# Twelve units of half products in the first feed-forward layer, four adaLN sums moved into the state-space groups, and part of the norm and the decays on the scalar engine

## The chip, the cores and the metric

The kernel runs on one core of a Trainium2 chip. The core has a matrix engine (TensorE, PE in the profile), a vector engine (VectorE, DVE), a scalar engine (ScalarE, ACT), GpSimd (POOL) and a queue engine that issues most of the transfers (SyncE, SP). Each runs its own list of instructions in order, and waits on semaphores for the others. The metric is device time in microseconds for one execution; less is better.

## The reference

A sequence of 512 tokens of width 1024 passes two layers. The first mixes tokens by a short gated convolution, the second by a Mamba-2 state-space mixer (SSD) with 8 groups of 4 heads. After each comes a SwiGLU feed-forward layer (FFN) of width 2816. Each of the four sub-layers is wrapped in RMS norms and adaLN vectors: shift, scale and gate, made from a conditioning vector c.

```python
mod = (jax.nn.silu(c) @ ada_w + ada_b).reshape(bsz, DEPTH, 2, 3, D_MODEL)
for i in range(DEPTH):
    shift, scale, gate = (mod[:, i, 0, k][:, None, :] for k in range(3))
    h = rmsnorm(x, norm_g[i, 0]) * (1.0 + scale) + shift
    y = short_conv_mixer(...) if i % 2 == 0 else ssd_mixer(...)
    x = x + gate * rmsnorm(y, norm_g[i, 1])
    shift, scale, gate = (mod[:, i, 1, k][:, None, :] for k in range(3))
    h = rmsnorm(x, norm_g[i, 2]) * (1.0 + scale) + shift
    gate_, up = jnp.split(h @ f_w_in[i], 2, axis=-1)
    x = x + gate * rmsnorm((jax.nn.silu(gate_) * up) @ f_w_out[i], norm_g[i, 3])
```

In the state-space mixer, h @ w_in gives z, the convolved x, B and C, and a step size dt; within chunks of 64 tokens the decay exp(cs_l - cs_s), masked to l >= s, weights C·B; y is multiplied by silu(z) and normalized per group: y * rsqrt(mean(y²) + eps) * norm_g.

## The kernel before

All products are float32 by three passes in a faster format: a value is split into a high and a low part (a copy on ScalarE, then a subtraction on VectorE), and high·high, high·low and low·high are summed in PSUM. Weights arrive from HBM in a staging tile (`wst`, `wsu`), are split into `whl`, and multiply the 512 tokens as moving data. A column tile of 128 outputs by 1024 inputs is a plain *chunk*: 8 x 3 = 24 matmuls of 128x512 (lines 285 to 287).

A *unit* (class Units, lines 577 on) does the same job for two column tiles with seven half-size products instead of eight (sums of weight blocks against sums of activation halves): 7 x 12 = 84 matmuls of 128x256 (line 654, into PSUM tiles sA, sB, sC). It needs sums of weight blocks: `fetch` (lines 599 to 612) issues per unit two loads into `sg`, three into `wsu` and two adding transfers on GpSimd's queue, and the unit before must have freed its staging tile.

The adaLN vectors are 12 sets of 1024 columns. Each set is eight 512 KB loads (`ada_st`, line 1004) with a multiply-add on VectorE for each (`ada_madd`, lines 122 to 127), a fold (L140), one small matmul with the constant `four` (`ada_fin`, L147, into PSUM tile `ada_ps`), four small additions on VectorE (L151), and for the gates a transposition through PSUM to DRAM and back (`put_gates`, L316 to L324).

In the first FFN, 6 units cover the first column tiles (12 of 44), and plain chunks in a loop over k the rest, with `sums(n)` steps (n multiply-adds) strewn in; then the down projection, `seq`. In the loop `x_load` also brings pieces for that projection. The second FFN has 16 units; in its units 0 to 8 `gate_late` makes the last set (its loads are L2249). The state-space mixer is a loop over groups g: VectorE, ScalarE and TensorE have their order written by hand. In one step of the loop TensorE projects columns of the group after (`nxt.project`, four chunks, `project_z`, two), transposes the current group's x (`xtok`), forms states and outputs (yo, yd), while VectorE applies convolution taps (L1678), subtracts the decays' arguments (`e_sub`, L1790, 16 small instructions), applies the norm of the group before (`root`, `norm`: ScalarE square root L1863, VectorE reciprocal L1867, L1870), splits weights (L231) and combines y (L1829 to L1832). The start of the loop's body, as it is written:

```python
conv2 = [nxt.project(i) for i in range(2)]
prev.root()
for q in range(2):
    cur.e_sub(q)
nxt.later[3][0]()
for q in range(2):
    cur.e_exp(q)
prev.norm()
next(conv2[0])
```

In the last group's step the output projection begins: its first 48 matmuls (L387) run while the group before is normalized, then come xtok and scores of the last group, and 48 more. T below counts from the start of a group's first chunk; 767.96 us is the one shown.

Of the kernel before, what the change touches and what calls it, by code (L numbers as in the profile page):

```python
# [16 lines left out]
P = 128  # L17
# [21 lines left out]
def trunk_kernel(  # L39
# [707 lines left out]
    ada_sets = [q0 * P for q0 in (16, 24, 32, 40, 48, 56, 64, 72, 80)]  # L747
# [4 lines left out]
    with ExitStack() as ph:  # L752
# [377 lines left out]
        UN1 = 6  # L1130
# [203 lines left out]
        with tc.manual_schedule(engines={PE_ENGINE, mybir.EngineType.SP, mybir.EngineType.Activation,  # L1334
# [6 lines left out]
            madds = ada_begin(6)  # L1341
# [111 lines left out]
            sums(3)  # L1453
# [4 lines left out]
            sums(3)  # L1458
# [25 lines left out]
            for k in range(k0, last + 1):  # L1484
                if k - k % 2 + 4 <= last:
                    load_pair_at(k - k % 2 + 4, k % 2)
                if k < k0 + 12:
                    x_load(*divmod(k - k0, 4))
# [13 lines left out]
                sums(1 if k in (k0 + 3, k0 + 8) else 2)  # L1502
# [19 lines left out]
            rows_g = put_gates(2, mm_ps)  # L1522
            next(rows_g)
# [15 lines left out]
            for q, item in enumerate(seq):  # L1539
# [6 lines left out]
                if q == 0:  # L1546
                    list(rows_g)
# [38 lines left out]
    with ExitStack() as ph:  # L1586
# [99 lines left out]
        class Group:  # L1686
# [96 lines left out]
            def e_sub(self, q):  # L1783

                e = self.e[:, 2 * q:2 * q + 2]
                for hh in range(2):
                    for cc in range(NCH):
                        sl = slice(cc * P, (cc + 1) * P)
                        hd = 4 * self.g + 2 * q + hh
                        dve.tensor_scalar(e[:, hh, sl], e[:, hh, sl], cs_tok[:, hd, cc:cc + 1], 0.0,  # L1790
                                          SUB, ALU.min)

            def e_exp(self, q):

                e = self.e[:, 2 * q:2 * q + 2]
                act.activation(e, e, AF.Exp)
# [64 lines left out]
            def root(self):  # L1861
                self.rg = t2("rg")
                act.activation(self.rg, self.ssg, AF.Sqrt, bias=eps_t, scale=1.0 / 256)  # L1863

            def norm(self):
                g = self.g
                dve.reciprocal(self.rg, self.rg)  # L1867
                for q in range(2):
                    y = ygs[2 * g + q]
                    dve.scalar_tensor_tensor(y, y, mng[:, 2 * g + q:2 * g + q + 1], self.rg, MUL, MUL)  # L1870

# [25 lines left out]
        with tc.manual_schedule(engines={PE_ENGINE, mybir.EngineType.Activation, mybir.EngineType.DVE}):  # L1897
            cur, nxt, nn = Group(0), Group(1), Group(2)
            nxt.weights(0)
            convs = [cur.conv(i, lead_ps[1 + i]) for i in range(4)]  # L1900
# [76 lines left out]
            for g in range(1, NG - 1):  # L1977
# [5 lines left out]
                for q in range(2):  # L1983
                    cur.e_sub(q)
                nxt.later[3][0]()
                for q in range(2):
                    cur.e_exp(q)
                prev.norm()
                next(conv2[0])
                next(conv2[0])  # L1990
                nxt.later[3][1]()
                nxt.weights(2)
                nxt.later[4][0]()
                next(conv2[1])
                cur.step_a()
                for q in range(2):
                    cur.e_mul(q)
                next(conv2[1])
                next(conv2[0])
                nxt.later[4][1]()  # L2000
# [10 lines left out]
                if nn:  # L2011
                    nn.weights(0)
                    nn.later[0][0]()
                cur.step_cc()
# [15 lines left out]

            prev, cur = cur, nxt
            next(parts[0])
            prev.root()
            for q in range(2):
                cur.e_sub(q)
            for q in range(2):
                cur.e_exp(q)
            prev.norm()
            ops = next(parts[0])
            for op in ops[:3]:  # L2040
                op()
            cur.step_a()
            for op in ops[3:]:
# [36 lines left out]
    with ExitStack() as ph:  # L2080
# [137 lines left out]
        with tc.manual_schedule(engines={PE_ENGINE, mybir.EngineType.SP, mybir.EngineType.Activation,  # L2218
# [19 lines left out]
            four = s1t[:, 6, 0:P]  # L2238
            make_four(four)

            def gate_late():

                st = [raw[:, 18 + 2 * b:20 + 2 * b, :].rearrange("p a b -> p (a b)") for b in range(2)]
                acc = s1t[:, 7:11, :].rearrange("p a b -> p (a b)")
                part = s1t[:, 6, P:P + 32]

                def load(k):
                    if k < KD:
                        dma(st[k % 2], ada_w[k * P:(k + 1) * P, 88 * P:96 * P])  # L2249

                load(0)
                load(1)
                yield
                for k in range(KD):
                    ada_madd(acc, st[k % 2], k)
                    load(k + 2)
                    yield
                ada_fold(acc, part)
                yield
                yield from ada_fin(88 * P, part)  # L2260
                yield from put_gates(3)

# [272 lines left out]
```

## Time and profile before

| what | us |
|---|---|
| median of three runs | 1335.93 |
| the runs | 1336.46, 1334.27, 1335.93 |
| profiled execution | 1334.83 |
| span of its profile | 1333.0 |

The span is one execution between the first and last instruction that the profiler saw; the rest of the profiled execution's time, 1.83 us, lies around it. Stages by the span's clock: convolution mixer to about 200 us, units of the first FFN about 250 to 308, its chunks 308 to 446, its down projection 453 to 548, state-space start from 590, groups 608 to 888 at 40 us each, output projection with the last group to 960, units of the second FFN 1032 to 1200, its remaining chunks and down projection to the end. Rows of a view have engine, line, operation and tiles as out<-in; a row of a timeline has start and length ahead of them.

### The profile page before, as it was taken

How to read it: one execution, taken by the hardware profiler on the slowest of the kernel's cores; microseconds unless marked ns; L12 is line 12 of the kernel's file. 1: busy time of each engine (PE TensorE's matmuls, PEld its weight loads, DVE VectorE, ACT ScalarE, POOL GpSimd, SP SyncE). 2: the span in 40 equal slices, each digit the busy share in tenths (PEclk: the TensorE clock that was granted, in tenths of full speed). 3: DMA queues.
4: the chain of work that ended last, by engine and by line, in shares of the span. 5: the costliest groups of instructions: out<-in, count | busy, mean ns of one | idle time of the engine just before them, and what ended most of it. 6: DMA issues, size and time to landing. Idle time of an engine off the chain costs nothing.

```text
span 1333.0 us, 19834 instructions
## 1 busy us (share of the span) xinstructions
PE 1314.0 (99%) x7653; PEld 1140.6 (86%) x7653; DVE 1049.6 (79%) x1627; ACT 662.4 (50%) x1084; POOL 99.5 (7%) x123
## 2 busy tenths in 40 slices
PE   8999999999999999999999999999999999999998
PEld 7788889998887788898888888888889999998886
DVE  5578767887876896769988989888678887776888
ACT  5333346453122565665554555554574545554665
POOL 0000000110000140000000000000001111100330
PEclk9999999999999999999999999999999999999999
DMA  9768651687898892414534243413343999869871
GB/s 311 235 199 255 226 171 41 180 220 240 280 300 277 240 182 64 130 33 145 159 111 138 70 140 111 143 64 126 104 126 80 237 237 235 209 174 287 178 137 63
DMA packets 209970, 228.53 MB, mean 171 GB/s; under 512 B 9668, under 2 KB 164180, under 8 KB 208852
## 3 DMA queue, kind: packets, MB, share of 16 engines
q1 hardware_dynamic: 191280, 187.88, 45.6%
q0 software_dynamic: 14448, 26.48, 11.4%
q10 hardware_dynamic: 4148, 12.90, 3.0%
q8 instruction: 60, 0.98, 0.3%
q14 instruction: 34, 0.28, 0.1%
HBM read 198.52 MB, written 2.24 MB: 151 GB/s over the span
## 4 chain that ended last, share of the span: by engine, by line
PE 74%; DMA 11%; DVE 8%; ACT 3%; issue 2%; SPq 2%; ACTq 0%; DVEq 0%; POOLq 0%
PE ip L285 10%; PE ip L287 10%; PE ip L286 10%; PE y L387 8%; PE sA L654 5%; PE cA L2215 4%; DMA wsu<-wsu 4%; DMA wst<-in_f_w_in_dram 4%; PE cA L1309 3%; PE sC L654 2%; PE li L285 2%; PE li L287 2%; PE li L286 2%; DVE ada_acc L127 2%; PE li L936 1%
## 5 line engine op out<-in xcount | busy, mean ns | idle before, releaser
L285 PE MATMUL ip<-h,whl 128*128 128x512 f32 x744 | 294.4, 396 | 0.8 <-ACT whl L1477 0.3
L287 PE MATMUL ip<-h,whl 128*128 128x512 f32 x744 | 290.7, 391 | 2.2 <-DVE whl L1478 2.1
L286 PE MATMUL ip<-h,whl 128*128 128x512 f32 x744 | 290.0, 390 | 0.0
L287 PEld LDWEIGHTS ip<-h,whl 128*128 128x128 f32 x744 | 139.7, 188 | 33.7 <-DVE whl L1478 4.4
L285 PEld LDWEIGHTS ip<-h,whl 128*128 128x128 f32 x744 | 139.8, 188 | 31.9 <-ACT whl L1477 2.3
L286 PEld LDWEIGHTS ip<-h,whl 128*128 128x128 f32 x744 | 139.9, 188 | 27.8
L654 PE MATMUL sA<-tq,whl 128*128 128x256 f32 x792 | 103.7, 285 | 3.4 <-DVE g L681 1.6
L231 DVE TENSOR_TENSOR whl<-wst,whl 128x1024 fp32r<-128x1024 f32 x70 | 84.8, 1219 | 24.7 <-ACT whl L230 24.7
L654 PEld LDWEIGHTS sA<-tq,whl 128*128 128x128 f32 x792 | 98.3, 192 | 5.7 <-DVE g L681 2.5
L387 PE MATMUL y<-whlo,ys 128*128 128x512 f32 x384 | 89.3, 392 | 0.0
L387 PEld LDWEIGHTS y<-whlo,ys 128*128 128x128 f32 x384 | 71.8, 188 | 15.8 <-issue 0.7
L127 DVE SCALAR_TENSOR_TENSOR ada_acc<-ada_st,csil,ada_acc 128x1024 f32<-128x1024 f32 x63 | 80.7, 1281 | 3.7 <-DMA ada_st<-in_ada_w_dram 2.9
L285 PE MATMUL li<-h,whl 128*128 128x256 f32 x288 | 83.3, 289 | 0.0
L287 PE MATMUL li<-h,whl 128*128 128x256 f32 x288 | 81.7, 284 | 0.0
L286 PE MATMUL li<-h,whl 128*128 128x256 f32 x288 | 81.6, 283 | 0.0
L230 ACT CAST whl<-wst 128x1024 fp32r<-128x1024 f32 x70 | 72.7, 1041 | 11.1 <-DMA wst<-in_f_w_in_dram 9.0
L617 DVE TENSOR_TENSOR whl<-wsu,whl 128x1024 fp32r<-128x1024 f32 x46 | 56.3, 1223 | 26.3 <-ACT whl L616 26.1
L1678 DVE SCALAR_TENSOR_TENSOR cu<-ip,cols,cu 128x511 f32<-128x511 f32 (+2 forms) x84 | 62.8, 747 | 3.9 <-ACT cu L1675 1.4
L2215 PE MATMUL cA<-whlo,ao 128*128 128x512 f32 x264 | 61.0, 390 | 0.4 <-DVE c L2448 0.2
L2215 PEld LDWEIGHTS cA<-whlo,ao 128*128 128x128 f32 x264 | 49.3, 188 | 11.5 <-ACT whlo L2180 1.2
L616 ACT CAST whl<-wsu 128x1024 fp32r<-128x1024 f32 x46 | 48.1, 1045 | 18.7 <-PE sB L654 7.8
L1228 POOL DMA_DIRECT2D sg<-sg x22 | 19.1, 870 | 486.4 <-DMA sg<-in_f_w_in_dram 297.6
(385 smaller groups left out, 2571.0 us busy)
## 6 DMA issues: line engine op xcount, KB each, us to landing
ada_st<-in_ada_w_dram SPq DMA_DIRECT2D x88, 512.0 KB, 5.4
wst<-in_m_w_in_dram SPq DMA_DIRECT2D x14, 1024.0 KB, 5.6
wsu<-in_f_w_in_dram SPq DMA_DIRECT2D x24, 512.0 KB, 4.9
sg<-in_f_w_in_dram SPq DMA_DIRECT2D x44, 256.0 KB, 3.9
wsu<-in_f_w_in_dram SPq DMA_DIRECT2D x44, 256.0 KB, 5.2
wst<-in_f_w_in_dram SPq DMA_DIRECT2D x22, 512.0 KB, 6.1
wst<-in_f_w_in_dram SPq DMA_DIRECT2D x10, 1024.0 KB, 5.4
wst<-in_m_w_in_dram SPq DMA_DIRECT2D x20, 512.0 KB, 5.5
```

Source lines behind the costliest of these rows:

```text
L127: dve.scalar_tensor_tensor(acc, w, csil[:, k:k + 1], acc, MUL, ADD)
L230: later.append((lambda sw=sw, w=w: act.copy(w[:, 0, :nk, :], sw), lambda sw=sw, w=w: dve.tensor_tensor(w[:, 1, :nk, :], sw, w[:, 0, :nk, : ...
L231: lambda sw=sw, w=w: dve.tensor_tensor(w[:, 1, :nk, :], sw, w[:, 0, :nk, :].bitcast(F32), SUB)))
L285: pe.matmul(dst, w_at(w, 0, kk), a[:, 0, sl], start=start, stop=False)
L286: pe.matmul(dst, w_at(w, 0, kk), a[:, 1, sl], start=False, stop=False)
L287: pe.matmul(dst, w_at(w, 1, kk), a[:, 0, sl], start=False, stop=stop)
L387: pe.matmul(pst, a[:, al, tk], wt[:, wl, kk, :], start=k == 0 and i == 0, stop=k == K - 1 and i == 2, skip_group_check=bool(held))
L616: act.copy(dst[:, 0], src)
L617: dve.tensor_tensor(dst[:, 1], src, dst[:, 0].bitcast(F32), SUB)
L654: pe.matmul(dst, w[:, wl, k0 + k, :], self.moving(q, k, al), skip_group_check=True, start=q in self.FIRST and k == 0 and i == 0, stop=k == ...
L1678: dve.scalar_tensor_tensor(u[:, sft:], pst[:, :T - sft], w[3 - sft], u[:, sft:], MUL, ADD)
L2215: pe.matmul(bank[r][sub], a[:, al, q, tk], w[:, hl, q, :], start=first and k == 0, stop=last and k == 2, skip_group_check=True)
```

## The change

The first FFN now has 12 units (`UN1`), so the loop of plain chunks has 8 steps left, and x_load's pieces are issued in the first six of them. Nine adaLN sets were made in the first layer's FFN and before; now six are, with sums() steps reduced accordingly. The second FFN's `gate_late` is gone, as is the `put_gates(2)` ahead of the first FFN's down projection. The four sets of columns 64, 72, 80 and 88 (units of 128) are summed in groups 1 to 6 of the state-space loop, six steps to a group. A step is `late(g, 1)`: if a set has its fold, one step of its finish (`late_end`: first the small matmul, then the four additions, then the gate's transposition), then one multiply-add or fold.

```diff
-    ada_sets = [q0 * P for q0 in (16, 24, 32, 40, 48, 56, 64, 72, 80)]
+    ada_sets = [q0 * P for q0 in (16, 24, 32, 40, 48, 56)]
...
-        UN1 = 6
+        UN1 = 12
...
-            madds = ada_begin(6)
+            madds = ada_begin(3)
...
-            sums(3)
+            sums(2)
...
-                if k < k0 + 12:
-                    x_load(*divmod(k - k0, 4))
+                if k < k0 + 6:
+                    for i in (0, 2):
+                        x_load((k - k0) % 3, i + (k - k0) // 3)
...
-                sums(1 if k in (k0 + 3, k0 + 8) else 2)
+                sums(1)
...
-            rows_g = put_gates(2, mm_ps)
-            next(rows_g)
...
-                        dve.tensor_scalar(e[:, hh, sl], e[:, hh, sl], cs_tok[:, hd, cc:cc + 1], 0.0,
-                                          SUB, ALU.min)
+                        act.activation(e[:, hh, sl], e[:, hh, sl], AF.Relu, bias=cs_tok[:, hd, cc:cc + 1],
+                                       scale=-1.0)
...
-                act.activation(e, e, AF.Exp)
+                act.activation(e, e, AF.Exp, scale=-1.0)
...
-                act.activation(self.rg, self.ssg, AF.Sqrt, bias=eps_t, scale=1.0 / 256)
+                act.activation(self.rg, self.ssg, AF.Ln, bias=eps_t, scale=1.0 / 256)
+                act.activation(self.rg, self.rg, AF.Exp, scale=-0.5)
...
-                dve.reciprocal(self.rg, self.rg)
...
+        def late_sums():
+
+            held = ysp.tile([P, 2, T], F32, tag="ys", name="four")
+            for q0 in (64, 72, 80, 88):
+                acc, st = flat(ysp.tile([P, 2, T], F32, tag="ys", name="ada_acc")), []
+
+                def load(k):
+                    if k < KD:
+                        st.append(flat(ysp.tile([P, 2, T], F32, tag="ys", name="ada_st")))
+                        dma(st[k], ada_w[k * P:(k + 1) * P, q0 * P:q0 * P + D])
+
+                load(0)
+                load(1)
+                if q0 == 64:
+                    yield held[:, 0, 0:P]
+                for k in range(KD):
+                    ada_madd(acc, st[k], k)
+                    load(k + 2)
+                    yield
+                part = held[:, 1, q0 % 32:q0 % 32 + 32]
+                ada_fold(acc, part)
+                fins_late.append(late_end(q0, part))
+                yield
+
+        def late_end(q0, part):
+            yield from ada_fin(q0 * P, part)
+            if q0 % 24 == 16:
+                yield from put_gates(q0 // 24)
+
+        fins_late = []
+
+        def late(g, n):
+            for _ in range(n):
+                if fins_late and next(fins_late[0], 0) == 0:
+                    fins_late.pop(0)
+                next(steps_late, None)
...
                 prev.root()
-                for q in range(2):
-                    cur.e_sub(q)
+                late(g, 2)
                 nxt.later[3][0]()
-                for q in range(2):
-                    cur.e_exp(q)
                 prev.norm()
+                late(g, 1)
                 next(conv2[0])
                 next(conv2[0])
+                cur.e_sub(0)
                 nxt.later[3][1]()
...
                 next(conv2[1])
+                cur.e_sub(1)
                 cur.step_a()
+                late(g, 1)
+                for q in range(2):
+                    cur.e_exp(q)
...
             prev.root()
-            for q in range(2):
-                cur.e_sub(q)
-            for q in range(2):
-                cur.e_exp(q)
+            for step in fins_late:
+                list(step)
             prev.norm()
...
-            late = gate_late()
-            next(late)
...
-                    next(late, None)
```

The orders of the engines, at three places. First VectorE at the start of group 4 (the step of the loop in which the second set is finished), in the kernel before:

```order
L1850 TENSOR_TENSOR sqs<-accg,sqs 128x512
L231 TENSOR_TENSOR whl<-wst,whl 128x1024
L1790 TENSOR_SCALAR csb<-csb,cs_tok 128x128 x16
L1867 RECIPROCAL rg<-rg 128x512
L1870 SCALAR_TENSOR_TENSOR yg_7089<-yg_7089,cols_91,rg 128x512
L1870 SCALAR_TENSOR_TENSOR yg_7106<-yg_7106,cols_91,rg 128x512
L1678 SCALAR_TENSOR_TENSOR cu<-ip,cols_93,cu 128x511
```

and in the changed kernel (`ada_acc` is the sum, `mods` the finished vectors, `yg` the group's outputs):

```order
L1847 TENSOR_TENSOR sqs<-accg,sqs 128x512
L231 TENSOR_TENSOR whl<-wst,whl 128x1024
L125 TENSOR_SCALAR ada_acc<-ada_st,csil 128x1024
L151 TENSOR_TENSOR mods<-ada_ps,cols_92 32x8 x4
L127 SCALAR_TENSOR_TENSOR ada_acc<-ada_st,csil,ada_acc 128x1024
L1867 SCALAR_TENSOR_TENSOR yg_7072<-yg_7072,cols_91,rg 128x512
L1867 SCALAR_TENSOR_TENSOR yg_7089<-yg_7089,cols_91,rg 128x512
L127 SCALAR_TENSOR_TENSOR ada_acc<-ada_st,csil,ada_acc 128x1024
L1675 SCALAR_TENSOR_TENSOR cu<-ip,cols_93,cu 128x511
```

The decays' 16 subtractions and the reciprocal have left, and a first sum step, the four additions of the second set and further sum steps stand ahead of and around the norm. Second, TensorE in the same step; the rows are the end of its second chunk and what follows:

```order
L285 MATMUL ip<-h_5080,whl 128x512
L286 MATMUL ip<-h_5080,whl 128x512
L287 MATMUL ip<-h_5080,whl 128x512
L147 MATMUL ada_ps<-four 128x32
L1738 MATMUL xtok<-ident,xs_6479 128x128
L1738 MATMUL xtok<-ident,xs_6480 128x128
```

The set's small matmul L147, which the four additions read, stands behind the two chunks; in the kernel before, xtok follows the chunks directly. Third, VectorE where the output projection begins, before:

```order
L1881 TENSOR_TENSOR ys<-yg_6128,ys 128x512
L1790 TENSOR_SCALAR csb<-csb,cs_tok 128x128 x16
L1867 RECIPROCAL rg<-rg 128x512
L1870 SCALAR_TENSOR_TENSOR yg_7732<-yg_7732,cols_91,rg 128x512
L1870 SCALAR_TENSOR_TENSOR yg_7749<-yg_7749,cols_91,rg 128x512
L213 TENSOR_TENSOR whlo<-wsto,whlo 128x1024 x2
L1881 TENSOR_TENSOR ys<-yg_6437,ys 128x512
```

and in the changed kernel (`gcol` is the gate column, `ggp` its transpose in PSUM, `whlo` and `ys` the split weights and values of the second set of 48):

```order
L1915 TENSOR_TENSOR ys<-yg_6396,ys 128x512
L151 TENSOR_TENSOR mods<-ada_ps,cols_92 32x8 x4
L158 TENSOR_TENSOR gcol<-mods,cols_91 128x8
L322 COPY gr<-ggp 8x128
L1867 SCALAR_TENSOR_TENSOR yg_8106<-yg_8106,cols_91,rg 128x512
L1867 SCALAR_TENSOR_TENSOR yg_8123<-yg_8123,cols_91,rg 128x512
L213 TENSOR_TENSOR whlo<-wsto,whlo 128x1024 x2
L1915 TENSOR_TENSOR ys<-yg_6731,ys 128x512
```

The last set's additions, gate column and copy now stand between the projection's first values and the norm of the last group but one. On TensorE their matmul L147 and the transposition L319 follow the first 48 matmuls:

```order
L387 MATMUL y_8219<-whlo,ys 128x512 x3
L147 MATMUL ada_ps<-four 128x32
L319 MATMUL ggp<-ident,gcol 8x128
L1738 MATMUL xtok<-ident,xs_7527 128x128
L1738 MATMUL xtok<-ident,xs_7528 128x128
```

The transposition needs the gate column from VectorE, and xtok, the scores and the second 48 matmuls come behind it.

36 lines of the change are left out of this document (12 added, 24 removed).

## The prediction, as put on record before the result was known

> **What bounds the kernel now.** The page first: its head and the chain that ended last.
>
> ```profile
> span 1333.0 us, 19834 instructions
> PE 1314.0 (99%) x7653; PEld 1140.6 (86%) x7653; DVE 1049.6 (79%) x1627; ACT 662.4 (50%) x1084; POOL 99.5 (7%) x123
> PE 74%; DMA 11%; DVE 8%; ACT 3%; issue 2%; SPq 2%; ACTq 0%; DVEq 0%; POOLq 0%
> ```
>
> TensorE is busy for 99% of the span, so time is won only by taking matmuls away or closing its few holes, and lost wherever it is made to wait. The mean hides the stages that the change touches, so next the windows: the half-product units of both FFNs, the plain chunks of the first, one state-space group, and the output projection. Columns: window, length, busy time of PE, PEld, DVE, ACT, POOL, granted clock, DMA share, GB/s.
>
> ```profile
> 255.60:305.90 50.30, 49.69 (x411) 49.18 (x410) 42.66 (x57) 25.83 (x43) 7.79 (x9) 1.00 0.85 221
> 390.00:446.00 56.00, 53.22 (x226) 41.21 (x225) 40.76 (x48) 16.87 (x22) 0.00 (x0) 1.00 0.79 264
> 768.00:808.00 40.00, 40.00 (x217) 33.74 (x216) 35.63 (x59) 21.19 (x28) 1.30 (x1) 1.00 0.39 118
> 888.00:954.00 66.00, 65.97 (x327) 54.21 (x326) 52.59 (x77) 33.03 (x45) 0.00 (x0) 1.00 0.33 104
> 1095.00:1130.00 35.00, 32.69 (x265) 31.73 (x264) 28.70 (x39) 16.92 (x31) 5.19 (x6) 1.00 0.92 232
> ```
>
> Three things stand there. A state-space group (40.00 us) leaves no hole in TensorE, but VectorE has only 4.4 us to spare, while ScalarE has 18.8 and DMA more than half. The chunks of the first FFN leave TensorE holes at a DMA share of 0.79. And the units of the second FFN, at 0.92, leave holes too.
>
> **The change part by part.** *Chunks to units.* The prices are distances of starts in the timeline: two plain chunks in a row, and units (the last two rows are cut short by the window asked for).
>
> ```profile
> 767.96 0.39 PE L285 MATMUL ip<-h,whl 128*128 128x512 f32 x1
> 773.40 0.39 PE L285 MATMUL ip<-h,whl 128*128 128x512 f32 x1
> ...
> 1085.61 1.60 PE L654 MATMUL sB<-h,whl 128*128 128x256 f32 x12
> 1095.68 1.60 PE L654 MATMUL sB<-h,whl 128*128 128x256 f32 x12
> 1107.20 1.60 PE L654 MATMUL sB<-h,whl 128*128 128x256 f32 x12
> 1118.36 1.60 PE L654 MATMUL sB<-h,whl 128*128 128x256 f32 x12
> 1129.44 1.00 PE L654 MATMUL sB<-h,whl 128*128 128x256 f32 x7
> 1139.74 0.64 PE L654 MATMUL sB<-h,whl 128*128 128x256 f32 x4
> ```
>
> A chunk is 24 matmuls in 5.44 us, so the two that a unit replaces cost 10.88. An unhindered unit, 84 half-wide matmuls, takes 10.07 (1085.61 to 1095.68). That is 0.81 each and 4.8 us for six. But the next four took 11.52, 11.16, 11.08 and 10.30. What they waited for:
>
> ```profile
> 1088.05 0.37 SPq L605 DMA_DIRECT2D wsu<-in_f_w_in_dram  x1
> 1099.78 0.37 SPq L605 DMA_DIRECT2D wsu<-in_f_w_in_dram  x1
> 1099.87 1.05 ACT L616 CAST whl<-wsu 128x1024 fp32r<-128x1024 f32 x1 [3.62 <-DMA wsu<-wsu]
> ...
> 297.99 0.37 SPq L605 DMA_DIRECT2D wsu<-in_f_w_in_dram  x1
> 305.86 1.60 PE L654 MATMUL sB<-h,whl 128*128 128x256 f32 x12
> ```
>
> Weight fetches of successive units (L605) come 11.73 us apart, slower than the 10.07 that a unit takes, and 1107.20 and 1118.36 follow their fetches by 19.1 and 18.6 us: that is how long fetch, sum, cast and subtraction take. The first FFN's fetch at 297.99 would, at a full pace, belong to a unit at 305.86 + 10.07 = 315.93, 17.9 us behind: too short, so the loop decides from there. Those fetches carry one 512 KB adaLN load per unit (as the second FFN's did), and the new units 6 to 11 keep it. So I give these six units 11.25 us each, between 10.07 and 11.52. Twelve chunks now cost 65.3 plus holes; the window 390 to 446 has 222 plain matmuls, 222 x 0.227 = 50.3 us, and about 0.5 of adaLN, so some 5.1 of its 56 us are lost to DMA. The twelve chunks are 70.4 with these. Six units at 11.25 make 67.5, less 0.5 where the hole of the last plain chunk closes: **-3.4 us**. Bounds: units at 10.07 give 60.4 and -10; units at 11.73, the fetch distance itself, give 70.4 and no gain.
>
> *Second FFN.* Eight 512 KB loads and nine VectorE steps leave its units. Over the 10.07 pace those four units lose 1.45 + 1.09 + 1.01 + 0.23 = 3.8; the last of these may stay, so **-3.7** (from -2.5, the first two alone, to -4.3, with half a microsecond of the other units).
>
> *State-space groups.* What leaves and enters VectorE, and ScalarE's sequence at a group's start:
>
> ```profile
> 766.40 3.22 DVE L1790 TENSOR_SCALAR csb<-csb,cs_tok 128x128 f32<-128x128 f32 x16
> 771.42 3.35 DVE L1867 RECIPROCAL rg<-rg 128x512 f32<-128x512 f32 x1 [1.80 <-ACT rg L1863]
> 776.34 2.32 DVE L1678 SCALAR_TENSOR_TENSOR cu<-ip,cols,cu 128x511 f32<-128x511 f32 x3
> ...
> 769.40 1.28 ACT L1863 ACT_TABLE_LOAD   x1 [1.10 <-issue]
> 770.70 0.69 ACT L1863 ACTIVATE rg<-ssg,eps 128x512 f32<-128x512 f32 x1
> 772.34 1.28 ACT L1796 ACT_TABLE_LOAD   x1
> 773.63 2.01 ACT L1796 ACTIVATE csb<-csb 128x1024 f32<-128x1024 f32 x2
> ...
> L125 DVE TENSOR_SCALAR ada_acc<-ada_st,csil x9: 746/750/754, 72.3 to 419.0; 128x1024 f32<-128x1024 f32 x9
> L127 DVE SCALAR_TENSOR_TENSOR ada_acc<-ada_st,csil,ada_acc 128x1024 f32<-128x1024 f32 x63 | 80.7, 1281 | 3.7 <-DMA ada_st<-in_ada_w_dram 2.9
> L140 DVE TRANSPOSE_TENSOR_REDUCE fold<-ada_acc 128x32 f32<-128x1024 f32 x9 | 11.2, 1245 | 0.3
> L151 DVE TENSOR_TENSOR mods<-ada_ps,cols x40: 144/162/173, 110.2 to 1148.2; 32x8 f32<-32x8 f32 x40
> ```
>
> VectorE loses 3.22 + 3.35 = 6.6 us a group and gains six sum steps in groups 1 to 6: 5 x 1.28 + 0.75 = 7.2. From 35.6 it goes to 36.2, and 36.9 with a finish of a set (4 x 0.16). So far under 40: that alone is free. ScalarE gains 16 128x128 activations, between an eighth of the 1.0 us of a 1024-wide one and the whole 0.69 of the 512-wide one; at 0.3 each and one activation of 0.69 for the root, 21.2 becomes about 27, hidden too. The norm waits until load, logarithm, load and exponential are over, T = 5.4 us into the group by these rows (table load from 769.40, then 1.28 + 0.69 + 1.28 + 0.69), but its reciprocal ended at T = 6.8 (771.42 + 3.35): no loss.
>
> The Trainium skill, "ScalarE: Activation LUTs", section "What ACT_TABLE_LOAD costs", counts a drain of some 1.4 us to each load beside its 1.28; here the next activation starts right behind the load (772.34 + 1.28 = 773.62), so no run here shows it, and by the page the sum would be up to 1.4 us a group larger where the norm comes last.
>
> What costs is the finishing of a set, where an instruction stands at the wrong place of a strict sequence. In group 4 the finish's four L151 come second on VectorE, behind the first sum step, and they read the matmul L147. On TensorE that stands behind both chunks that the group begins with, that is 2 x 5.44 = 10.88 us into the group:
>
> ```profile
> 778.84 1.04 PE L1741 MATMUL xtok<-ident,xs 128*128 128x128 f32 x8
> 753.16 1.50 PE L1813 MATMUL yo<-ct,prev 128*128 128x128 f32 x12
> 754.59 1.97 PE L1824 MATMUL yd<-csb,xdt 128*64 128x128 f32 x32
> ...
>   PE ada_ps L147: 6.4, 1
> ```
>
> (778.84 is 10.88 behind 767.96; the last row, of what L151 waited for, shows that such a wait already happened once in the second FFN, 6.4 us.) Queued behind L151 are the norm, the taps of chunk 0 and all that follows. VectorE then does 0.75 us of work before T = 11.1 and 36.9 - 0.75 = 36.2 after it: the group ends at 47.3, **+7.3**. Bounds: +4, if groups 5 and 6 with 3 us of slack each recover part of it before TensorE notices, and +9.5 if the late loads behind it add 2. In group 2 the finish stands after the scores and costs nothing by itself, but the gate's transpose takes one of the auxiliary banks, and the copy that frees it stands far down VectorE's sequence: the second yd, ready at T = 27.6 (754.59 less 727.96, the group before, plus 1.0), gets its bank when y1 is read, T = 29.9: **+2.3** (0 to +3). In groups 1, 3 and 6 a sum step asks for a load that was issued only one step earlier: a few tenths each, +0.9 together, and 1.8 more that VectorE is late by when the output projection starts: **+2.7** (0 to +5).
>
> The tail, from the chain of waits:
>
> ```profile
> 888.16 10.88 PE y L387 x48
> 899.04 0.87 PE xtok L1741 x8
> 901.14 10.93 PE y L387 x48
> ```
>
> VectorE there normalizes the group before the last at 896.41, and the second set of y matmuls follows 4.73 us later.
>
> ```profile
> 896.41 1.41 DVE L1870 SCALAR_TENSOR_TENSOR yg<-yg,cols,rg 128x512 f32<-128x512 f32 x2
> ```
>
> Now the last set's finish comes ahead of that norm, and its L147 stands behind the 48 matmuls: 888.16 + 10.88 = 899.04, then matmul, four L151, gate column, transpose and copy, some 1.5 us at 0.2 to 0.3 for each that isn't an L151: norm at 900.6 and not 896.41, **+4.2** (+3 to +5).
>
> The groups together: 7.3 + 2.3 + 2.7 + 4.2 = **+16.5** (+11 to +19). The loads' own traffic is not the trouble there: 36 x 512 KB over 240 us add 79 GB/s to 118, where the window of the chunks moved 264.
>
> Sum: -3.4 - 3.7 + 16.5 = +9.4; against the profiled execution's 1334.83 that is 1344.2. The median of the runs shown is 1335.93, 1.1 above that execution, so the forecast is **1345.0 us**.
>
> **The rivals.** *VectorE's delay compounds, 1350* (chance 0.2). If group 4's delay makes loads of weights and decays late (they wait for buffers that VectorE frees), groups 5 and 6 lose some 2 us each, and the units run at the fetch distance of 11.73, no gain: 1345 + 2 + 3 = 1350. For it: six sum steps leave VectorE 3 us of slack only. Against it: the DMA share of 0.39.
>
> *The units keep their pace, 1338* (0.12). If fetches are no longer slowed by what surrounded them, the first FFN gains 10 and not 3.4: 1345 - 6.6 = 1338.4. For it: 255.60 to 305.90, with TensorE busy 49.69 of 50.30 and one sum load per unit from the third on. Against it: the fetch distance of 11.73 with just that load.
>
> *TensorE does not feel VectorE's delay, 1335* (0.08), the case that is not slower. VectorE's slack is 40 - 36.2 = 3.8 us in each group; over groups 4 to 6 that is 11.4, more than the 7.3 of group 4 and the 2.7 of the late loads. If TensorE's chunks, whose weights are split a chunk or more ahead, can stand in for the work that comes late, both terms vanish: 1345.0 - 10.0 = 1335.0. It decides from the point where a chunk's lead in weights exceeds the delay. For it: TensorE without a hole in the group. Against it: the matmuls of the states wait for xw and those of yo for prev, both made by VectorE behind the L151, and a chunk is only 5.4 us of cover.
>
> *The finishes hide entirely* (0.03), that is, the matmul L147 comes before the chunks on the chip: group 4 and the tail cost nothing, 1345 - 7.3 - 4.2 = 1333.5. Against it: TensorE runs its list in order in each view above.
>
> **How the numbers follow.** The forecast has 0.57; its own range, from the terms' bounds, is 1341 to 1348. With 1350 at 0.2, 1338 at 0.12 and 0.11 between 1333 and 1335, the range that holds eight in ten is 1336 to 1351. A measurement of this kernel can't tell less than 0.2%, 2.7 us, from no change, so "faster" means under 1333.3 and "slower" over 1338.6. Faster: half of the last rival, and four or five hundredths where two of the low cases meet, 0.06. Same: the rest of the last two rivals and most of 1338, half of which lies above the bound, 0.12. Slower: the forecast, 1350 and that half, 0.82.
>
> **What would show it.** In the profile after: L151 of group 4 idle for about 9 us on PE ada_ps; that group 47 us long, group 2 about 42, others 40 to 41; second y set 17 us behind the first, not 13; starts of the first FFN's units 11.2 us apart from the seventh on; no hole in the second FFN's units 7 to 10; ACT loads still three per group. Wrong it would be if the units of the first FFN lie 10.1 apart (then about 1338), or if TensorE's matmuls near the finishes show no wait longer than 2 us (then no more than 1335).

## The result and the profile after

| | before | changed |
|---|---|---|
| median, us | 1335.10 | 1347.33 |
| lowest to highest, us | 1332.97 to 1336.46 | 1345.70 to 1350.47 |
| runs | 4 | 4 |
| ratio to before, 95% interval | | 1.0096 (1.0072 to 1.0120) |
| profiled execution, span, us | 1333.0 | 1348.7 |

The changed kernel is slower by 12.2 us, and the time lies 2.3 us above the forecast. The profile shown is that of the changed kernel's longest execution, 1350.47 us; where the other profiles of nearly the same code differ, it is said. Its head and the chain that ended last:

```profile
span 1348.7 us, 20425 instructions
PE 1316.2 (98%) x7869; PEld 1152.9 (85%) x7869; DVE 1021.3 (76%) x1533; ACT 722.9 (54%) x1258; POOL 108.0 (8%) x135
PE 73%; DVE 11%; DMA 8%; ACT 4%; issue 3%; ACTq 0%; SPq 0%; POOL 0%; DVEq 0%; POOLq 0%
```

VectorE does 28 us less in all and stands on the chain for 11% of the span instead of 8%. It was relieved on average and became the last to arrive at a few places. The windows of the stages (columns as in the prediction): the sixth to the eleventh unit of the first FFN, group 4, the output projection with the last group, and the units of the second FFN that had holes.

```profile
306.00:376.00 70.00, 64.53 (x522) 62.81 (x521) 54.66 (x78) 32.62 (x56) 9.51 (x11) 1.00 0.87 221
771.80:819.50 47.70, 42.36 (x217) 35.24 (x217) 37.10 (x52) 26.18 (x44) 1.31 (x1) 0.96 0.56 168
891.50:957.00 65.50, 60.84 (x294) 48.81 (x293) 44.13 (x66) 38.67 (x63) 1.29 (x1) 0.97 0.28 94
1095.00:1150.00 55.00, 55.00 (x461) 55.00 (x460) 40.16 (x58) 28.67 (x49) 10.34 (x12) 1.00 0.86 215
```

The same work of a group, 217 matmuls, now takes 47.7 us with 5.3 us of holes, and ScalarE has gone to 26 us, about as estimated. The holes of the second FFN's units are gone.

All stages at once are told by the starts of a few TensorE instructions. The table has, from the timelines, the time from the first unit's sB to the first matmul of the down projection (cA) in each FFN, the steps from the xtok of group 0, 1, ... 6 to that of the next group, and the time from the last xtok to the last y. It holds the experiments too, which are described below.

| kernel | first FFN | steps of groups 0 to 6 | last group and projection | second FFN | span |
|---|---|---|---|---|---|
| before | 197.1 | 40.0, 40.0, 40.0, 40.0, 40.0, 40.0, 40.0 | 85.5 | 184.7 | 1333.0 |
| changed | 194.1 | 40.4, 44.5, 42.1, 40.5, 47.8, 40.3, 44.2 | 89.3 | 180.8 | 1348.7 |
| e1_group4 | 193.2 | 40.1, 44.8, 42.0, 41.1, 44.5, 40.3, 44.0 | 89.0 | 180.8 | 1344.0 |
| e2_tail | 192.2 | 40.2, 44.3, 42.0, 40.7, 49.0, 40.3, 44.3 | 87.5 | 180.8 | 1346.0 |
| e3_third | 194.6 | 40.0, 40.3, 42.1, 40.1, 47.6, 40.3, 42.7 | 89.0 | 180.8 | 1342.1 |
| e4_units | 189.5 | 40.6, 43.1, 42.0, 40.4, 49.0, 40.3, 45.7 | 88.3 | 180.8 | 1344.5 |
| e5_fins | 192.4 | 40.1, 40.2, 40.3, 40.2, 40.3, 40.3, 41.6 | 85.0 | 180.8 | 1325.6 |
| e6_all | 187.8 | 40.0, 40.3, 40.3, 40.2, 40.3, 40.3, 41.6 | 85.2 | 180.8 | 1321.5 |
| e7_dve | 191.0 | 41.9, 46.9, 44.3, 45.2, 43.8, 43.3, 45.9 | 85.1 | 180.8 | 1353.7 |

From before to changed the FFNs give 3.0 and 3.9 us, the seven steps of the groups take 19.8 more, and the last group with the projection 3.8 more. Another 1.1 us is gained between the first FFN's down projection and group 0, which no term of the forecast had and no run takes apart; what is left, 0.2, lies before and behind.

Where VectorE waited in the groups, the three largest sums (us in total, times, longest):

```profile
DVE mods L151 <- PE ada_ps L147: 19.0, 2, 9.8
DVE yg L1867 <- ACT rg L1861: 15.8, 5, 4.8
DVE ada_acc L127 <- DMA ada_st<-in_ada_w_dram: 6.1, 3, 3.1
```

The first line is the forecast's main term: two waits of over 9 us for the small matmul, one in group 4 and one in the last group. In group 4, VectorE's timeline, and TensorE's 16 us later:

```profile
772.27 0.75 DVE L125 TENSOR_SCALAR ada_acc<-ada_st,csil 128x1024 f32<-128x1024 f32 x1
782.86 0.69 DVE L151 TENSOR_TENSOR mods<-ada_ps,cols 32x8 f32<-32x8 f32 x4 [9.83 <-PE ada_ps L147]
...
802.52 0.49 PE L1810 MATMUL yo<-ct,prev 128*128 128x128 f32 x2 [3.67 <-DVE prev L1778]
```

The sum step, then 9.83 us of nothing, then the four additions. VectorE hardly stops after that, and 16 us later TensorE has run out of work that doesn't need it: yo waits 3.67 us for prev. In the last group the chain of waits runs right through the finish:

```profile
903.03 10.73 PE y L387 x46
913.76 0.15 PE ada_ps L147 x2
913.93 0.15 DVE mods L151
...
914.66 0.18 DVE gcol L158
914.84 0.04 issue
914.88 0.29 PE ggp L319
...
915.40 1.39 DVE yg L1867 x2
916.79 2.27 DVE whlo L213 x2
919.06 0.61 DVE ys L1915
919.67 0.04 issue
919.72 5.30 PE y L387 x15
```

Projection, small matmul, additions, gate column, transposition, norm, splits, projection: one behind the other, 16.7 us from the start of the first set (903.0; two matmuls of it went ahead at 901.5) to that of the second, where before it was 12.98.

Group 1 shows what the forecast priced too low, a late load. VectorE's third sum step there, and the piece of the chain ahead of it:

```profile
655.86 1.29 DVE L127 SCALAR_TENSOR_TENSOR ada_acc<-ada_st,csil,ada_acc 128x1024 f32<-128x1024 f32 x1 [3.14 <-DMA ada_st<-in_ada_w_dram]
...
646.68 0.37 SPq L221
647.16 8.61 DMA ada_st<-in_ada_w_dram
```

The load is issued right behind weights of the next group (L221, 1 MB) and lands after 8.6 us, where the median of these loads in the profile before is 5.4; everything on VectorE behind it moves by 3.1 us. Where the profile gives the landing of such a load in the groups, it took 3.5 to 12.0 us, 7.8 in the median. That the weights ahead of it are what makes this one late was not tested by itself.

### The profile page after: what moved, and what is told of

Its sections match the earlier page's. It is cut to its first block, busy times and chain, and to the rows that moved or that the text cites. A ratio compares the mean times of both kernels' runs of the same rounds, so it can differ in the third digit from the quotient of the medians.

```text
span 1348.7 us, 20425 instructions
## 1 busy us (share of the span) xinstructions
PE 1316.2 (98%) x7869; PEld 1152.9 (85%) x7869; DVE 1021.3 (76%) x1533; ACT 722.9 (54%) x1258; POOL 108.0 (8%) x135
## 3 DMA queue, kind: packets, MB, share of 16 engines
q0 software_dynamic: 16176, 29.63, 12.7%
## 4 chain that ended last, share of the span: by engine, by line
PE 73%; DVE 11%; DMA 8%; ACT 4%; issue 3%; ACTq 0%; SPq 0%; POOL 0%; DVEq 0%; POOLq 0%
PE y L387 8%; PE ip L285 8%; PE ip L286 8%; PE ip L287 8%; PE sA L654 7%; PE cA L2260 4%; DMA wsu<-wsu 4%; PE sC L654 4%; PE cA L1309 3%; PE li L285 3%; PE li L287 3%; PE li L286 3%; PE li L936 2%; DVE cu L1675 2%; DMA ada_st<-in_ada_w_dram 2%
## 5 line engine op out<-in xcount | busy, mean ns | idle before, releaser
L285 PE MATMUL ip<-h,whl 128*128 128x512 f32 x648 | 256.0, 395 | 0.2 <-DVE cv L1035 0.2
L287 PE MATMUL ip<-h,whl 128*128 128x512 f32 x648 | 252.4, 390 | 0.0
L286 PE MATMUL ip<-h,whl 128*128 128x512 f32 x648 | 252.3, 389 | 0.0
L285 PEld LDWEIGHTS ip<-h,whl 128*128 128x128 f32 x648 | 121.7, 188 | 26.3 <-issue 1.8
L287 PEld LDWEIGHTS ip<-h,whl 128*128 128x128 f32 x648 | 121.6, 188 | 25.8
L286 PEld LDWEIGHTS ip<-h,whl 128*128 128x128 f32 x648 | 121.8, 188 | 24.3
L654 PE MATMUL sA<-tq,whl 128*128 128x256 f32 x1008 | 131.8, 284 | 7.0 <-DVE raw L681 3.4
L654 PEld LDWEIGHTS sA<-tq,whl 128*128 128x128 f32 x1008 | 125.1, 192 | 10.0 <-DVE g L681 4.3
L617 DVE TENSOR_TENSOR whl<-wsu,whl 128x1024 fp32r<-128x1024 f32 x58 | 70.9, 1223 | 42.1 <-ACT whl L616 42.1
L127 DVE SCALAR_TENSOR_TENSOR ada_acc<-ada_st,csil,ada_acc 128x1024 f32<-128x1024 f32 x70 | 89.7, 1281 | 6.7 <-DMA ada_st<-in_ada_w_dram 6.1
L616 ACT CAST whl<-wsu 128x1024 fp32r<-128x1024 f32 x58 | 60.7, 1047 | 27.7 <-DMA wsu<-wsu 9.0
L1228 POOL DMA_DIRECT2D sg<-sg x28 | 24.3, 869 | 537.8 <-DVE whl L213 226.9
L2260 PEld LDWEIGHTS cA<-whlo,ao 128*128 128x128 f32 x264 | 49.3, 188 | 11.6 <-ACT whlo L2225 1.2
```

What stands on the lines that cost most here:

```text
L127: dve.scalar_tensor_tensor(acc, w, csil[:, k:k + 1], acc, MUL, ADD)
L285: pe.matmul(dst, w_at(w, 0, kk), a[:, 0, sl], start=start, stop=False)
L286: pe.matmul(dst, w_at(w, 0, kk), a[:, 1, sl], start=False, stop=False)
L287: pe.matmul(dst, w_at(w, 1, kk), a[:, 0, sl], start=False, stop=stop)
L616: act.copy(dst[:, 0], src)
L617: dve.tensor_tensor(dst[:, 1], src, dst[:, 0].bitcast(F32), SUB)
```

## The experiments

Four single edits to the changed kernel, each at one of the places named above, and three kernels built from them. The four single edits ran once each, beside one run of the kernel before (1335.0 us), and e7_dve ran once too, so their verdict is read from the steps in the table and from the rows. The three others ran beside twelve runs of the kernel before, with a median of 1333.46 us.

**e1_group4.** The small matmul ahead of the two chunks.

```diff
                 nxt.e, nxt.ecs = decays(g + 1)
+                if g == 4:
+                    next(fins_late[0])
                 conv2 = [nxt.project(i) for i in range(2)]
```

> One edit to the changed kernel: in group 4 the small matmul L147 of the second set is issued ahead of the group's two chunks; the four additions stay where they are. Theory (in-order wait): the step from the xtok of group 4 to that of group 5, 47.7 us in the changed kernel, falls to 40.2 to 41.0, VectorE's 9.8 us on PE ada_ps in that group and TensorE's 3.7 us on prev vanish, the granted clock there is 1.00, and the run is 7 us shorter, about 1340 to 1342. Rival (VectorE has too much to do in a group with six sum steps and a finish): the step stays at 44 us or more, since the same instructions are left. The other groups as before.

One run: 1345.88 us, over the 1340 to 1342 expected. The wait for ada_ps in group 4 is gone (L151 runs at once, at 771.35), but the step is 44.5 us, not 40.2 to 41.0, and 1.7 us of it are still lost to a lower granted clock. That is the rival's number, but not for its reason. What VectorE waits for instead:

```profile
782.15 1.28 DVE L127 SCALAR_TENSOR_TENSOR ada_acc<-ada_st,csil,ada_acc 128x1024 f32<-128x1024 f32 x1 [4.92 <-DMA ada_st<-in_ada_w_dram]
```

It is group 1's late load again, in group 4, where the longer wait for the matmul had hidden it. So 3.3 us of the 7.8 belong to the matmul's place alone, and the rest only comes free if the load does; e5_fins, which has both, is at 40.3.

**e2_tail.** In the last group, the matmul ahead of the first 48 of the projection, the rest of the finish behind the norm.

```diff
             prev, cur = cur, nxt
+            for step in fins_late:
+                next(step)
             next(parts[0])
             prev.root()
+            prev.norm()
             for step in fins_late:
-                list(step)
-            prev.norm()
+                next(step)
...
             cur.step_a()
+            for step in fins_late:
+                list(step)
             cur.e_sub(1)
```

> One edit to the changed kernel: in the last group's step the matmul L147 of the last set is issued ahead of the 48 matmuls of the output projection, its additions behind the norm, and the gate's transposition and copy behind the scores. Theory: the second 48 matmuls follow the first by 12.9 to 13.6 us and not by 16.7, VectorE's 9.2 us on PE ada_ps there vanish, and the run is 3.5 to 5 us shorter, about 1343 to 1344. Rival (VectorE is late there because of the work in the groups before, not because of the finish): the distance stays above 15.5.

One run: 1347.74 us, which says little, since group 4's step came out 1.2 us longer in this execution. The column of the last group falls by 1.8 us, from 89.3 to 87.5, half of what was expected, and group 6's step, which holds the first 48 matmuls, stays at 44.3. From the main part of the first set (901.96) to the second (916.23) it is 14.3 us, not the 12.9 to 13.6 expected; but from 902.95 on the clock is at half for 3.4 us, which costs 1.7. So the second 48 now start in time, as far as the finish goes, and stop after twelve. TensorE, then ScalarE:

```profile
916.23 3.02 PE L387 MATMUL y<-whlo,ys 128*128 128x512 f32 x12
920.79 8.73 PE L387 MATMUL y<-whlo,ys 128*128 128x512 f32 x36 [1.54 <-ACT ys L1914]
...
915.89 2.45 ACT L1787 ACTIVATE csb<-csb,cs_tok 128x128 f32<-128x128 f32 x8
918.24 1.99 ACT L1793 ACTIVATE csb<-csb 128x1024 f32<-128x1024 f32 x2
920.13 1.65 ACT L1914 CAST ys<-yg 128x512 fp32r<-128x512 f32 x3
```

The casts of ys that the matmuls need stand on ScalarE behind eight of the subtractions that came from VectorE, and behind the exponential. The first wait had covered a second one, and that one is the price of the move to ScalarE at this place. They could change places in the list, which the fifth kernel does.

**e3_third.** The third sum step later.

```diff
                 prev.norm()
-                late(g, 1)
                 next(conv2[0])
                 next(conv2[0])
                 cur.e_sub(0)
                 nxt.later[3][1]()
+                late(g, 1)
```

> One edit to the changed kernel: the third sum step of each group stands behind the taps of the first chunk and a weight subtraction, not right behind the norm; 3.5 us more for its load. Theory (the load is issued late behind 1 MB of weights and VectorE idles for it): VectorE's waits for ada_st in groups 1, 3 and 6 (3.1, 1.3, 1.7 us) shrink to under 0.5 each, the step from xtok of group 1 to that of group 2 falls from 44.5 to under 41.5, its clock back to 1.00, run 3 to 4 us shorter. Rival (group 1 is late through its first groups' ScalarE sequence): the step stays above 43.

One run: 1343.86 us. Group 1's step falls from 44.5 to 40.3, that of group 6 from 44.2 to 42.7, and group 3's from 40.5 to 40.1: 6.1 us for a line that moved, 1.7 of it clock, since group 1 has no hole left that lowers it. No wait of VectorE for ada_st is left. The rival is out.

**e4_units.** Units 7 to 11 of the first FFN, counted from 0, without adaLN steps and loads.

```diff
-                    sums(1)
+                    sums(1 if u < 7 else 0)
...
-                sums(1)
+                sums(2 if k == k0 else 1)
```

> One edit to the changed kernel: units 7 to 11 of the first FFN carry no adaLN step and so no 512 KB load; the five steps go to the plain chunks behind. Theory (that load slows the weight fetch of the unit loop): units 8 to 11 come 10.1 to 10.5 us apart and not 11.4, chunks lose under 1 us of it, run 3 to 5 us shorter, about 1343. Rival (the adding transfers on GpSimd's queue or VectorE set the unit's pace): they stay 11 us and more apart and the run is unchanged within 1 us.

One run: 1346.86 us, not about 1343, in part since groups 4 and 6 took 49.0 and 45.7 us in this execution. The first FFN's column falls to 189.5, where the changed kernel and the three runs above have 192.2 to 194.6: about 4 us less, as expected. The spacing of units 8 to 11 was half a miss: 10.6, 10.8, 11.2 and 10.2 us. The fetches tell why. Theirs in the changed kernel, and in e6_all, which has the same edit:

```profile
321.18 0.37 SPq L605 DMA_DIRECT2D wsu<-in_f_w_in_dram  x1
332.28 0.37 SPq L605 DMA_DIRECT2D wsu<-in_f_w_in_dram  x1
343.89 0.37 SPq L605 DMA_DIRECT2D wsu<-in_f_w_in_dram  x1
```

```profile
330.17 0.37 SPq L605 DMA_DIRECT2D wsu<-in_f_w_in_dram  x1
339.61 0.37 SPq L605 DMA_DIRECT2D wsu<-in_f_w_in_dram  x1
348.64 0.37 SPq L605 DMA_DIRECT2D wsu<-in_f_w_in_dram  x1
```

11.1 and 11.6 us apart with the load, 9.4 and 9.0 without. The load is the cause of this distance: behind 330 us it is 10.7 to 12.1 us in all six profiles that have the load, and 8.5 to 10.1 in the two that don't. But a unit follows its fetch by some 18.5 us, so the units that stood to gain first had been fetched before it was gone. How much of the 4 us the load costs these profiles can't tell. Ahead of the first load that is missing all eight run the same code, and there alone the two steps from the sixth to the eighth unit scatter from 21.4 to 25.4 us. From the eighth unit to cA it is 117.2 us here and 116.1 in e6_all, and 116.8 to 120.7 in the six with the load.

**e5_fins.** All finishes by one rule: their TensorE part ahead of a group's chunks, their VectorE part behind the norm; the later third step; and in the last group the ys casts ahead of the second half of the subtractions.

```diff
         def late(g, n):
             for _ in range(n):
-                if fins_late and next(fins_late[0], 0) == 0:
-                    fins_late.pop(0)
                 next(steps_late, None)
+
+        def fin():
+            while fins_late and next(fins_late[0], 0) == 0:
+                fins_late.pop(0)
...
+                fin()
                 conv2 = [nxt.project(i) for i in range(2)]
...
                 prev.norm()
-                late(g, 1)
+                fin()
...
                 nxt.later[3][1]()
+                late(g, 1)
...
             prev, cur = cur, nxt
+            fin()
             next(parts[0])
             prev.root()
-            for step in fins_late:
-                list(step)
             prev.norm()
+            fin()
...
             cur.step_a()
-            cur.e_sub(1)
-            for q in range(2):
-                cur.e_exp(q)
+            fin()
             for op in ops[3:]:
                 op()
+            cur.e_sub(1)
+            for q in range(2):
+                cur.e_exp(q)
+            fin()
```

> The changed kernel with every finish of a set placed for the in-order lists: its TensorE part (small matmul, transposition) ahead of a group's two chunks, its VectorE part behind the norm; the third sum step later as in the run on it; in the last group's step the ys casts ahead of the second half of the decays. Theory (all of the loss in the groups is waits for a misplaced instruction or a late load): the steps between the xtok of groups are 40.0 to 40.6 each but the last (41 to 42.5), the second set of 48 matmuls follows the first by 13 to 14 us, TensorE's clock is 1.00 throughout, and the time is 1327 to 1331, faster than before. Rival (part of the loss is the load of six sum steps and 16 activations itself): steps of 41 us and more in groups 1 to 6, time 1335 or above.

Median 1327.72 us (5 runs), ratio to the kernel before 0.9964 (0.9952 to 0.9977): faster. Windows of two groups and of the projection, and the only wait of TensorE over 0.5 us between 600 and 960 us:

```profile
644.00:684.00 40.00, 40.00 (x216) 33.45 (x215) 37.66 (x49) 27.14 (x47) 1.30 (x1) 1.00 0.63 197
764.00:804.30 40.30, 40.30 (x219) 33.98 (x218) 36.29 (x48) 26.23 (x44) 1.29 (x1) 1.00 0.63 201
890.00:956.00 66.00, 65.97 (x328) 54.29 (x327) 44.14 (x64) 37.20 (x61) 0.00 (x0) 1.00 0.31 104
...
PE y L387 <- DVE ys L1917: 0.8, 1, 0.8
```

The work is that of the changed kernel, VectorE's 36 to 38 us of 40 included, and the groups take 40.0 to 40.3. So six sum steps a group do fit. The main part of the second 48 follows that of the first by 12.7 us. Group 2's step also falls, from 42.1 to 40.3, with the transposition at its new place.

**e6_all.** e5_fins with the edit of e4_units.

> The run before this one, and units 7 to 11 without adaLN steps. Theory: 3 to 4 us less again, 1324 to 1328, ratio to the kernel before 0.992 to 0.995. Rival (the gain of those units is taken back by the plain chunks once nothing else is late): same time as the run before this one within 1 us.

Median 1325.16 us (6 runs), ratio to the kernel before 0.9941 (0.9929 to 0.9954), the fastest of all kernels here. The first FFN's column is 4.6 us under that of e5_fins in the profiles, but 4.0 of these lie between the sixth and the eighth unit, ahead of the first load that is missing. The medians differ by 2.6 us, a little less than expected; this is the measure of the edit, of few runs, whose ranges meet at 1327 to 1328 us.

**e7_dve.** e5_fins with the subtractions and the reciprocal back on VectorE.

```diff
-                        act.activation(e[:, hh, sl], e[:, hh, sl], AF.Relu, bias=cs_tok[:, hd, cc:cc + 1],
-                                       scale=-1.0)
+                        dve.tensor_scalar(e[:, hh, sl], e[:, hh, sl], cs_tok[:, hd, cc:cc + 1], 0.0,
+                                          SUB, ALU.min)
...
-                act.activation(e, e, AF.Exp, scale=-1.0)
+                act.activation(e, e, AF.Exp)
...
-                act.activation(self.rg, self.ssg, AF.Ln, bias=eps_t, scale=1.0 / 256)
-                act.activation(self.rg, self.rg, AF.Exp, scale=-0.5)
+                act.activation(self.rg, self.ssg, AF.Sqrt, bias=eps_t, scale=1.0 / 256)
...
+                dve.reciprocal(self.rg, self.rg)
```

> The placed version with the decays' subtractions and the reciprocal back on VectorE, that is without the move to ScalarE. Theory (VectorE's budget of 40 us a group is what the move makes room for): VectorE would need 36.2 + 6.6 = 42.8 us a group, the steps in groups 1 to 6 are 42 to 44 us, 12 to 20 us more than the placed version, about 1345. Rival (the move was not needed, VectorE's busy time overstates what binds): 40 to 41 us each and the time of the placed version within 3 us.

One run: 1356.41 us, 28.7 above e5_fins and more than either theory gave. Windows of 44 us in two places, and TensorE's main wait:

```profile
660.00:704.00 44.00, 40.13 (x204) 33.52 (x203) 41.39 (x63) 19.59 (x26) 1.29 (x1) 0.92 0.53 167
790.00:834.00 44.00, 41.58 (x219) 34.25 (x219) 43.16 (x69) 20.80 (x27) 1.29 (x1) 1.00 0.56 172
...
PE yo L1810 <- DVE prev L1778: 13.9, 14, 3.7
```

VectorE is full and TensorE waits for prev. The steps of 43 to 44 are what 42.8 us of VectorE's work gives; the larger ones have holes with a lower clock behind them (0.92 in the first window): of the 28.3 us that the seven steps take more than in e5_fins, 8.5 are lost to the clock, and the 19.8 that are left are the theory's upper end. The order is that of e5_fins, in which the subtractions stand later than in the kernel before, so this prices the move at these places, not at every possible one.

## Why the prediction was right

**First FFN, -3.4 forecast.** Measured -3.0 in this profile, -2.5 to -6.1 in the five others with the same code there. The argument from the fetch distance held: the six steps from the sixth unit to the twelfth are 10.3 to 12.3 us, 11.4 on average where 11.25 was forecast, and the plain chunks behind have lost their holes. That the load in the unit is the cause was an inference then; e4_units and e6_all show it for the fetch distance. What the load costs in time rests on the 2.6 us between the medians of e5_fins and e6_all.

**Second FFN, -3.7 forecast.** Measured -3.9: units 7 to 10 are 10.1 us apart like those around them.

**Group 4, +7.3 forecast.** Measured +7.8, by the mechanism named, VectorE idle 9.83 us on ada_ps. The sum was made up otherwise, though: TensorE's holes are 5.3 us, about 1.7 are, by the granted clock, TensorE running slowly behind the largest of them, and 0.8 is left over. And the waits overlap: e1_group4 took only 3.3 us of it away, since a late load lay under it.

**Group 2, +2.3 forecast.** Measured +2.1; the second yd waited for the bank:

```profile
PE yd L1821 <- DVE y L1826: 1.5, 1, 1.5
```

**Late loads, +0.9 forecast: the term that was mis-sized.** The prediction gave "a few tenths each" to groups 1, 3 and 6 and showed no working for it. Group 1 alone is +4.5: VectorE waits 3.1 us for a load that lands after 8.6 us, TensorE stands still for 2.3 us in its turn, and again some 1.7 are clock. e3_third settles it: the three groups are 6.1 us shorter with the third step moved. The sign "others 40 to 41" failed in groups 1 and 6.

**The tail, +4.2 and the 1.8 of lateness.** Measured 4.2 in step 6 and 3.8 behind it, 8.0 in all. Of these 1.7 are clock, and 1.5 of step 6 are the late load of group 6, by e3_third; the 4.8 that are left stand beside the 6.0 forecast. The finish by itself, from the first set to the second, is 16.7 us where it was 13.0, 3.7 beside the 4.2 forecast.

**What was missing: the clock.** Three times 1.7, or 5.1 us, of the groups' 23.6 are lost to a lower granted clock after holes; no term of the sum had that. Without it the groups come to 18.5, beside 16.5 forecast. The profiled span therefore grew by 15.7 and not by 9.4; the median of four runs, among which this execution was the longest, grew by 12.2.

**Luck in the number.** The mechanisms named for both FFNs, for groups 2 and 4 and for the tail are those that the traces show. That the time came within 2.3 us is in part luck: the clock was 5.1 us that nobody had counted, the late loads were 3.5 more than forecast even without it, and groups 2 and 4 and the tail came out 2.6 under their terms.

**The norm on ScalarE, nothing forecast.** Right for the time, since e5_fins keeps it and has groups of 40.0 to 40.3. It isn't idle-free: VectorE waited 15.8 us in five groups for rg, time that it had to spare. ScalarE's rows at such a place, in group 1:

```profile
647.35 1.28 ACT L1860 ACT_TABLE_LOAD   x1
648.64 0.69 ACT L1860 ACTIVATE rg<-ssg,eps 128x512 f32<-128x512 f32 x1
649.35 1.28 ACT L1861 ACT_TABLE_LOAD   x1
650.64 0.63 ACT L1861 ACTIVATE rg<-rg 128x512 f32<-128x512 f32 x1
```

The Trainium skill, "ScalarE: Activation LUTs", section "What ACT_TABLE_LOAD costs", would put a drain of 1.38 us to each load; the activations start 0.01 us behind the loads here, so the measurement decides: 1.28 us a load. Ahead of four of the eight loads for the logarithm ScalarE idled some 1.1 us that the profile puts down to nothing; the loads for the exponential follow at once.

**The rivals.** "VectorE's delay compounds" had loads of weights and decays late behind group 4; late were the loads of the sums, and groups 3 and 5 stayed at 40.5 and 40.3, so it does not compound. The measured 1347.3 us lies about midway between the forecast and that rival's 1350, so the time alone would not have told. "The units keep their pace" and the two cases near 1335 did not happen. That the finishes hide (near 1334) takes a different order; e5_fins has one, and goes lower still, at 1327.7.

## What to carry to other kernels

Work moved into a stage with room on average must also be placed: in lists that run in order, a tiny instruction that reads another engine's result costs as much as what stands ahead of its producer there (four additions of 0.16 us cost 9.8 us of VectorE). Ask for each cross-engine pair where the producer stands, and issue it ahead of the long work and its consumer behind. Where a wait is removed, expect the one under it: two of the four single edits returned about half of what the wait had seemed to cost and uncovered the next one, and only the edits together gave the rest back.

## What the runs showed of the hardware

A hole of 1 to 3.7 us on TensorE is often, not always, followed by several microseconds at a lower granted clock. Windows of the changed kernel: the hole of group 1 and what follows, and that of group 4.

```profile
670.40:672.16 1.76, 0.00 (x0) 0.00 (x0) 1.62 (x4) 0.55 (x1) 0.00 (x0) 1.00 0.55 123
672.16:680.00 7.84, 7.34 (x52) 6.38 (x53) 7.60 (x11) 1.57 (x2) 0.00 (x0) 0.78 0.41 122
798.90:802.50 3.60, 0.00 (x0) 0.00 (x0) 3.46 (x5) 0.55 (x1) 0.00 (x0) 1.00 0.25 59
802.50:811.00 8.50, 7.98 (x55) 6.90 (x56) 8.25 (x13) 2.03 (x3) 0.00 (x0) 0.80 0.45 135
...
674.42 3.40 PE L1821 MATMUL yd<-csb,xdt 128*64 128x128 f32 x32
```

At 0.78 over 7.84 us, 1.7 us are lost; the 32 matmuls of yd take 3.40 us, where the kernel before needed 1.97. A hole of 3.7 us had it behind it in all five profiles that have one. One of 1.6 us at the same place of group 1 had none (e4_units, whose step there is 43.1 and not 44.5), and in e2_tail and e4_units group 4 was 49.0 us long.

The traces show what this scatter hangs on. From the first units to the end of the projection every lowered stretch is at half clock, and 3.41 us long or twice that. In one profile the stretches start whole multiples of 3.413 us apart: here at 673.99, 803.69 and 919.75, 38 and 34 multiples. So there is a fixed grid in time, and it lies otherwise in each execution. The rows show the grid's windows at group 1's hole, two of the changed kernel and two of e4_units:

```profile
670.58:673.99 3.41, 1.33 (x9) 1.14 (x10) 3.13 (x7) 0.37 (x1) 0.00 (x0) 1.00 0.51 154
673.99:677.40 3.41, 3.41 (x31) 3.19 (x32) 3.37 (x4) 1.57 (x2) 0.00 (x0) 0.50 0.00 0
...
663.80:667.21 3.41, 2.18 (x11) 1.68 (x9) 3.31 (x5) 0.78 (x1) 0.00 (x0) 1.00 0.21 29
667.21:670.62 3.41, 2.54 (x28) 2.23 (x30) 3.20 (x6) 0.00 (x0) 0.00 (x0) 1.00 0.32 125
```

In the changed kernel TensorE idles 2.1 us of one window, and the next is at half clock. In e4_units the hole is split between two windows, 1.2 and 0.9 us, and nothing follows. Counted over the eight profiles with the change, from 250 us on, TensorE idled 1.6 us or more in 22 windows, and behind 20 of them the next was at half clock; the other two had 1.7 and 1.8 us. No window with less made the clock fall, and behind three of the longer holes it stayed at half for two windows. So a short hole costs its length plus 0, 1.7 or 3.4 us, by how it falls on the grid. It is not shown that this widens the spread of the runs: the four of the changed kernel lie 4.8 us apart, but the twelve of the kernel before lie 5.2. The Trainium skill, "TensorE: Matmul & The Clock Gate", Part 1, tells of a free-running window of 3.4 us that must pass idle for the clock to fall; the grid agrees with such a window, but here about half of one idle was enough.
